# Splitting the first a loads and regrouping the last stores of a batched matmul

## The chip, the cores and the metric

The kernel runs on one core of a Trainium2 chip. The metric is the device time of one execution, in microseconds. The kernel before takes 133.37 us, the median of three runs (133.36, 133.37, 133.55).

## The reference

```python
def setup_inputs():
    return {"a": np.random.randn(1024, 64, 64).astype(np.float32),
            "b": np.random.randn(1024, 64, 64).astype(np.float32)}

def reference(a, b):
    return np.matmul(a, b).astype(np.float32)
```

It is a batch of 1024 products of 64 x 64 matrices. The two inputs are 16.8 MB each, and so is the output, in fp32: 50.3 MB in all for 0.5 GFLOP. The kernel computes in bf16 and accumulates in fp32.

## The kernel before, in words

**Tiles.** The batch is cut into 16 tiles of 64 matrices for b and the output (index t, 1 MB each), and into 8 tiles of 128 matrices for a (index s, 2 MB each, so one a tile serves two t). An a tile is loaded in four parts (h = 0 to 3), each of 32 matrices: a partition holds 16 rows of one matrix, so that four partitions make a matrix, and a part is 128 partitions of 4 KB. In the source the four partitions of a matrix lie 4 KB apart and the next matrix of the part lies 64 KB on. An address pattern for a whole part therefore has an outer dimension of 32 matrices and an inner one of 4.

**Who loads.** For a tiles 1 to 7, GpSimd loads three of the four parts and turns them into bf16 on the way (`cast_load_a`, L73), and SyncE loads the fourth as fp32 (`load_a`, L81). The first a tile is different (`load_first_a`, L84 to L95): all four parts come as fp32, two on SyncE's queue and two on ScalarE's, and land in two buffers of the output pool. A b tile is one load of 1 MB (`load_b`, L100), on SyncE's queue for even t and ScalarE's for odd t, three tiles ahead.

**From a tile to product.** The a tile is cast to bf16 and regrouped (`regroup`, L109 for the first tile, L112 and L115 later; L129 on the path for tiles 1 to 3). It is transposed, on TensorE (`transpose`, L141, copied out by ScalarE in L144) or on VectorE for a tiles 1 to 3 (`transpose_dve`, L131). VectorE then writes it into a block-diagonal operand (`spread`, L157 or L167), so that four matrices share one pass through the 128 x 128 array. The b tile is cast to bf16 (`cast`, L176; the last tile in four pieces, L181 and L183). TensorE multiplies (L221) into PSUM, and ScalarE, with VectorE's help for some tiles, copies the result to an output tile `o_sb` of 128 partitions and 8 KB (`evacuate`, L209). The last tile is multiplied and copied in four quarters, the first and third by ScalarE, the second and fourth by VectorE.

**Stores.** `multiply` does not issue the stores itself: it leaves them in `held`, and `store(t)` issues them one tile later, after the next `multiply` (HOLD is 2). `put(lo, n)` (L198) stores n of the eight column groups of a tile, on the queue that `store_queue` names: GpSimd's for tiles 0 to 14, ScalarE's and SyncE's in turn for tile 15. Tiles 0 to 13 go as one store of 1 MB. Tile 14 goes as two of 512 KB, tile 15 as four of 256 KB.

**What sets the order.** The order is written out by hand (`tc.manual_schedule()`); every engine does its instructions in the order in which the program lists them. At the start SyncE issues two parts of the first a tile, b tile 0, the a_raw part of tile 1, b tile 2 and so on; ScalarE issues two parts of the first a tile, loads its function table, and issues b tile 1; GpSimd issues the three cast loads of a tile 1, builds the identity, clears an operand and goes on to further cast loads. At the end the order is: multiply tile 15, store tile 14, store tile 15. The profile calls GpSimd's DMA queue q0, SyncE's q1 and ScalarE's q10.

Of the kernel before, what the change touches and what calls it, by code (L numbers as in the profile page):

```python
# [13 lines left out]
def kernel(  # L14
# [14 lines left out]
    nc = tc.nc  # L29
# [4 lines left out]
    n_t, n_s = B // 64, B // 128  # L34
# [6 lines left out]
    a_v = a.rearrange("(s g h) (mp v) k -> s h g mp (v k)", h=4, g=32, v=16)  # L41
# [21 lines left out]
    held = {}  # L63

    def store_queue(t, lo):
        if t < n_t - 1:
            return nc.gpsimd
        return nc.scalar if lo % 4 == 0 else nc.sync

    def cast_load_a(s):  # L70
        a_sb = a_pool.tile([128, 3, 16, 64], bf16, name="a_sb")
# [12 lines left out]
    def load_first_a():  # L84

        raw = [
            o_pool.tile([128, 8, 2, 2, 64], fp32, name="o_sb")[:].rearrange(
                "p gh j wl n -> p (gh j wl n)"
            )
            for _ in range(2)  # L90
        ]
        parts = [raw[h % 2][:, 1024 * (h // 2) : 1024 * (h // 2) + 1024] for h in range(4)]
        for h in range(4):
            (nc.scalar if h % 2 else nc.sync).dma_start(out=parts[h], in_=a_v[0, h])  # L94
        a_tiles[0] = parts  # L95

    def load_b(t):
# [92 lines left out]
    def multiply(t):  # L190
        at_bd = bd_tiles[t % N_BD][:].rearrange("p g (j wl) h mp vo -> p j g (wl h mp vo)", j=2)
        at_bd = at_bd.bitcast(bf16).rearrange("p j g (c u) -> p j g c u", u=2)
        b_bf = bbf_tiles.pop(t)
        last = t == n_t - 1
        o_sb = o_pool.tile([128, 8, 2, 2, 64], fp32, name="o_sb")

        def put(lo, n):
            store_queue(t, lo).dma_start(  # L198
                out=o_v[t, :, lo : lo + n, :],
                in_=o_sb[:, lo : lo + n].rearrange("p gh j wl n -> p (gh j wl n)"),  # L200
            )

        def evacuate(o_ps, gh, n, copies):

            for par in range(2):
                for wl in range(2):
                    src = o_ps[64 * wl : 64 * wl + 64, :, par, :, :]
                    dst = o_sb[64 * par : 64 * par + 64, gh : gh + n, :, wl, :]
                    copies[2 * par + wl](dst, src)  # L209

        for half in range(2):
            if not last:
                o_ps = o_psum.tile([128, 4, 2, 2, 64], fp32, name="o_ps")
            for g8 in range(8):
                if last and g8 % 4 == 0:
                    o_ps = t_psum.tile([128, 2, 2, 2, 64], fp32, name="at_ps")
                g = 8 * half + g8
                gl = (g8 % 4 if last else g8) // 2
                for j in range(2):
                    for u in range(2):  # L220
                        nc.tensor.matmul(  # L221
                            o_ps[:, gl, g % 2, j, :],
                            at_bd[:, j, g, :, u],
                            b_bf[:, g, 64 * u : 64 * u + 64],
                            start=(u == 0),
                            stop=(u == 1),
                        )
                if last and g8 % 4 == 3:
                    copy = nc.scalar.copy if g8 == 3 else nc.vector.tensor_copy
                    evacuate(o_ps, g // 4 * 2, 2, [copy] * 4)  # L230
            if not last:
                copies = [nc.scalar.copy] * 4
                if half and t % 2 and t > 2 * max(ON_DVE):
                    copies[2:] = [nc.vector.tensor_copy] * 2
                evacuate(o_ps, 4 * half, 4, copies)
        if last:
            held[t] = [lambda q=q: put(2 * q, 2) for q in range(4)]
        else:
            whole = t < n_t - 2
            held[t] = [lambda q=q: put(q, 8 if whole else 4) for q in ([0] if whole else [0, 4])]  # L240

    with tc.manual_schedule():
        first_cast = cast_load_a(1)
        load_first_a()

        nc.vector.memset(warm[:, 0:1], 0.0)
# [15 lines left out]
        for t in range(n_t):  # L262
            s, half = t // 2, t % 2
            if t + 1 < n_t:
                spread(t + 1)
                cast(t + 1)
            if t + B_AHEAD < n_t:
                load_b(t + B_AHEAD)
            if half == 0 and 0 < s < n_s - 1 - A_AHEAD:
                load_a(s + 1 + A_AHEAD)  # L270
            if half == 0 and 0 < s < n_s - 1 and s + 1 not in ON_DVE:
                transpose(s + 1, 1)
            multiply(t)
            if t == 0:
                transpose_dve(1, 0)
                transpose_dve(1, 1)
                a_tiles.pop(1)
                load_a(A_AHEAD)
                load_a(A_AHEAD + 1)
            if t and s + 2 in ON_DVE and (half or s):  # L280
                for part in [0, 1] if t == 1 else [half]:
                    transpose_dve(s + 2, part)
                if half:
                    a_tiles.pop(s + 2)
            elif half == 0 and 0 < s and s + 2 < n_s:
                regroup(s + 2)
            elif half == 1 and s + 2 < n_s:
                transpose(s + 2, 0)
            if t >= HOLD - 1:
                store(t - HOLD + 1)  # L290
# [32 lines left out]
```

## Time and profile before

| What | Value |
| --- | --- |
| median of three runs | 133.37 us |
| profiled execution, its own time | 133.69 us |
| its span, first to last instruction | 131.8 us |
| HBM read and written | 33.55 MB and 16.78 MB, 382 GB/s over the span |
| busy: TensorE 60.3, VectorE 102.0, ScalarE 88.1, GpSimd 33.2 us | 46%, 77%, 67%, 25% of the span |
| DMA queues q0, q1, q10 | 52.7%, 28.5%, 20.2% of 16 engines' span |
| whole stores of 1 MB, issue to landing | 21.5 us (median of 14) |
| first a loads, issue to landing | 6.8 us on SyncE, 7.5 us on ScalarE (medians of two) |

The span is the time between the first and the last instruction that the profile holds; the execution's own time is longer by what lies around it. "DMA" in the page's slices is the mean busy share of the core's 16 DMA engines, in tenths. A queue's share is the time of its packets over 16 engines' span. GB/s counts what was written, so a load that turns fp32 into bf16 counts half. A DMA is issued by an engine's instruction, and its packets follow later; "landing" is when the last of them has been acknowledged.

### The profile page before, as it was taken

The page shows a single profiled execution, that of the slowest core. Times are in us where ns is not written, and L with a number is a line of the kernel's source. Part 1 is how long each engine was busy: PE and PEld are TensorE (multiplying, and loading weights), DVE is VectorE, ACT ScalarE, POOL GpSimd, SP SyncE. Part 2 cuts the span into 40 slices and gives each one's busy share as a digit, 9 for nine tenths or more (in the row PEclk, how much of TensorE's full clock was granted, in tenths as well). Part 3 has the DMA queues.
Part 4 walks back from the last instruction along what each step waited for, and adds up shares of the span by engine and source line. Part 5 has one row for each costly group of instructions (what it writes and reads, how often), then busy time and mean ns, then how long its engine had stood idle before and what let it go on. Part 6 is the DMA issues. An engine that isn't in the chain of part 4 may idle for free.

```text
span 131.8 us, 2749 instructions
## 1 busy us (share of the span) xinstructions
PE 60.3 (46%) x1104; PEld 57.2 (43%) x1104; DVE 102.0 (77%) x144; ACT 88.1 (67%) x158; POOL 33.2 (25%) x45
## 2 busy tenths in 40 slices
PE   0003701964090270908971983199369615366000
PEld 0003501964090270908961963198368614355000
DVE  5932099807999996999999999599999997798300
ACT  2123605599949069492999989559969998339930
POOL 6991000042016300618120204300420212041200
PEclk9999999999999998555599599559968999679755
DMA  3999999999999999999999999999999999999993
GB/s 71 344 341 306 306 306 297 270 313 319 328 316 401 347 310 308 399 390 395 314 288 364 400 397 359 306 303 389 393 390 392 395 391 393 391 405 402 402 379 135
DMA packets 18252, 44.99 MB, mean 341 GB/s; under 512 B 1088, under 2 KB 2112, under 8 KB 18240
## 3 DMA queue, kind: packets, MB, share of 16 engines
q0 software_dynamic: 7120, 21.24, 52.7%
q1 hardware_dynamic: 6064, 13.63, 28.5%
q10 hardware_dynamic: 5056, 9.96, 20.2%
q8 instruction: 8, 0.13, 0.4%
q14 instruction: 4, 0.03, 0.1%
HBM read 33.55 MB, written 16.78 MB: 382 GB/s over the span
## 4 chain that ended last, share of the span: by engine, by line
DMA 53%; ACT 16%; DVE 14%; PE 6%; issue 5%; SPq 2%; DVEq 0%; ACTq 0%
DMA b_sb<-in_b_dram 53%; ACT o_sb L209 13%; PE o_ps L221 5%; DVE at_bd L167 4%; DVE b_bf L176 4%; DVE at_bd L157 2%; ACT b_bf L176 1%; DVE at_sb L131 1%; DVE o_sb L209 1%; DVE a_bf L112 1%; SPq L94 1%; ACT a_bf L129 1%; SPq L100 1%; ACT b_bf L183 1%; DVE a_bf L115 0%
## 5 line engine op out<-in xcount | busy, mean ns | idle before, releaser
L209 ACT COPY o_sb<-o_ps 64x512 f32<-64x512 f32 x112 | 65.0, 581 | 18.5 <-PE o_ps L221 14.3
L221 PEld LDWEIGHTS <-at_bd 128*128 128x128 bf16 x1024 | 45.3, 117 | 51.5 <-DVE b_bf L176 39.6
L221 PE MATMUL o_ps<-b_bf,at_bd 128*128 128x64 bf16 x960 | 45.7, 223 | 47.1 <-DVE b_bf L176 36.8
L167 DVE COPY at_bd<-at_sb 32x1024 f32<-32x1024 f32 x40 | 29.5, 737 | 5.9 <-ACT at_sb L144 4.9
L198 POOL DMA_DIRECT2D out_dram<-o_sb x16 | 17.1, 1068 | 53.8 <-ACT at_sb L144 21.1
L157 DVE COPY at_bd<-at_sb 32x512 f32<-32x512 f32 x48 | 21.6, 451 | 1.1
L73 POOL DMA_DIRECT2D a_sb<-in_a_dram x21 | 12.0, 588 | 37.2 <-DVE at_sb L131 34.0
L176 DVE CAST b_bf<-b_sb 128x2048 bf16<-128x2048 f32 x14 | 17.4, 1245 | 4.3 <-DMA b_sb<-in_b_dram 4.0
L141 PE MATMUL at_ps<-identity,a_bf 128*128 128x128 f32 x80 | 13.3, 336 | 11.9 <-ACT a_bf L109 11.9
L141 PEld LDWEIGHTS at_ps<-identity,a_bf 128*128 128x128 f32 x80 | 12.2, 181 | 11.9 <-issue 11.9
L144 ACT COPY at_sb<-at_ps 128x512 f32<-128x512 f32 x20 | 10.8, 591 | 2.4 <-PE at_ps L141 2.0
L131 DVE STREAM_TRANSPOSE at_sb<-a_sb 128x512 f32<-128x512 f32 x9 | 8.7, 1055 | 0.0
L131 DVE STREAM_TRANSPOSE at_sb<-a_bf 128x512 f32<-128x512 f32 x3 | 3.1, 1044 | 4.6 <-ACT a_bf L129 4.6
L109 ACT CAST a_bf<-o_sb 128x1024 bf16<-128x1024 f32 x2 | 2.1, 1045 | 5.9 <-DMA o_sb<-in_a_dram 5.9
L209 DVE COPY o_sb<-o_ps 64x512 f32<-64x512 f32 x8 | 5.5, 689 | 0.2
L109 DVE CAST a_bf<-o_sb 128x1024 bf16<-128x1024 f32 x2 | 3.2, 1599 | 2.9 <-DMA o_sb<-in_a_dram 2.9
L176 ACT CAST b_bf<-b_sb 128x2048 bf16<-128x2048 f32 x1 | 1.9, 1899 | 4.5 <-DMA b_sb<-in_b_dram 4.5
L112 DVE COPY a_bf<-a_sb 128x3072 bf16<-128x3072 bf16 x4 | 4.2, 1046 | 0.0
L183 ACT CAST b_bf<-b_sb 128x512 bf16<-128x512 f32 x2 | 1.1, 614 | 4.5 <-DMA b_sb<-in_b_dram 4.5
L250 DVE MEMSET at_bd<- 128x4096 f32 x1 | 3.5, 3472 | 0.8 <-issue 0.8
L209 DVE COPY o_sb<-at_ps 64x256 f32<-64x256 f32 x8 | 3.4, 422 | 0.5 <-PE at_ps L221 0.4
L129 ACT CAST a_bf<-a_raw 128x1024 bf16<-128x1024 f32 x3 | 3.1, 1045 | 0.1
(16 smaller groups left out, 15.4 us busy)
## 6 DMA issues: line engine op xcount, KB each, us to landing
out_dram<-o_sb POOLq DMA_DIRECT2D x14, 1024.0 KB, 21.5
a_sb<-in_a_dram POOLq DMA_DIRECT2D x21, 256.0 KB, 14.2
a_raw<-in_a_dram SPq DMA_DIRECT2D x7, 512.0 KB, 17.5
o_sb<-in_a_dram SPq DMA_DIRECT2D x2, 512.0 KB, 6.8
o_sb<-in_a_dram ACTq DMA_DIRECT2D x2, 512.0 KB, 7.5
out_dram<-o_sb POOLq DMA_DIRECT2D x2, 512.0 KB, 5.9
out_dram<-o_sb SPq DMA_DIRECT2D x2, 256.0 KB, 4.6
out_dram<-o_sb ACTq DMA_DIRECT2D x2, 256.0 KB, 4.6
```

The source lines that it names most:

```text
L73: nc.gpsimd.dma_start(out=a_sb[:, h, :, :].rearrange("p v k -> p (v k)"), in_=a_v[s, h], single_packet=True)
L109: copy(a_bf[:, :, h, :], a_sb[h].rearrange("p (v k) -> p v k", v=16))
L112: nc.vector.tensor_copy(a_bf[:, :, 0:3, :], cast_sb[:].rearrange("p h v k -> p v h k"))
L131: nc.vector.transpose(at_tiles[s][:, h].rearrange("p g w mp vo -> p w vo g mp"), pairs.rearrange("p (vo w kp) -> p w vo kp", vo=4, w=4),)
L141: nc.tensor.transpose(at_ps[:, vo, :], a_cols[:, 4 * vo + 2 * j + wl, :], identity[:])
L144: nc.scalar.copy(at_tiles[s][:, :, 2 * j + wl, :, :], at_ps[:].rearrange("p vo (g mp) -> p g mp vo", mp=4),)
L157: nc.vector.tensor_copy(bd[rows, 8 * i : 8 * i + 8, :, h, :, :].rearrange("p g w mp vo -> p (g w) (mp vo)"), at_sb[block : block + 32, h]. ...
L167: nc.vector.tensor_copy(bd[rows, :, :, h, :, :].rearrange("p g w mp vo -> p (g w) (mp vo)"), at_sb[rows, half].rearrange("p g w mp vo -> p ...
L176: (nc.vector.tensor_copy if t else nc.scalar.copy)(b_bf[:], b_sb[:])
L198: store_queue(t, lo).dma_start(out=o_v[t, :, lo : lo + n, :], in_=o_sb[:, lo : lo + n].rearrange("p gh j wl n -> p (gh j wl n)"),)
L209: copies[2 * par + wl](dst, src)
L221: nc.tensor.matmul(o_ps[:, gl, g % 2, j, :], at_bd[:, j, g, :, u], b_bf[:, g, 64 * u : 64 * u + 64], start=(u == 0), stop=(u == 1),)
```

## The change

It has two parts. At the start, each of the four loads of the first a tile becomes two: the first 8 matrices (32 partitions) and the other 24 (96 partitions), one behind the other on the same queue. At the end, tile 14 is stored whole, in one store of 1 MB on GpSimd's queue, and tile 15 in two: column groups 0 to 5 (768 KB) on GpSimd's queue, groups 6 and 7 (256 KB) on SyncE's. ScalarE issues no store any more.

```diff
     def store_queue(t, lo):
         if t < n_t - 1:
             return nc.gpsimd
-        return nc.scalar if lo % 4 == 0 else nc.sync
+        return nc.gpsimd if lo == 0 else nc.sync
...
         for h in range(4):
-            (nc.scalar if h % 2 else nc.sync).dma_start(out=parts[h], in_=a_v[0, h])
+            queue = nc.scalar if h % 2 else nc.sync
+            for lo, hi in ((0, 8), (8, 32)):
+                queue.dma_start(out=parts[h][4 * lo : 4 * hi], in_=a_v[0, h, lo:hi])
         a_tiles[0] = parts
...
         if last:
-            held[t] = [lambda q=q: put(2 * q, 2) for q in range(4)]
+            held[t] = [lambda: put(0, 6), lambda: put(6, 2)]
         else:
-            whole = t < n_t - 2
-            held[t] = [lambda q=q: put(q, 8 if whole else 4) for q in ([0] if whole else [0, 4])]
+            held[t] = [lambda: put(0, 8)]
```

## The prediction

> **What bounds the kernel now.** I read first the page's 40 slices and its queue table, then the stretches (DMA share and GB/s), the chain, the order of time at both ends, and the queues' packets in short stretches. From the page:
>
> ```profile
> span 131.8 us, 2749 instructions
> DMA  3999999999999999999999999999999999999993
> DMA packets 18252, 44.99 MB, mean 341 GB/s; under 512 B 1088, under 2 KB 2112, under 8 KB 18240
> q0 software_dynamic: 7120, 21.24, 52.7%
> q1 hardware_dynamic: 6064, 13.63, 28.5%
> q10 hardware_dynamic: 5056, 9.96, 20.2%
> DMA 53%; ACT 16%; DVE 14%; PE 6%; issue 5%; SPq 2%; DVEq 0%; ACTq 0%
> ```
>
> The 16 DMA engines are full from the second slice to the last but one; the three queues (q0 GpSimd's, q1 SyncE's, q10 ScalarE's) make up 101% of 16 engines' span. The chain is 53% waits for a b load, and each of those loads is long because it shares the engines. The small packets, 1088, are 16 for each of the kernel's 68 DMAs. The stretches show where the DMA work stops being full:
>
> ```profile
> 2.00:3.00 1.00, 0.00 (x0) 0.00 (x0) 1.00 (x1) 0.67 (x2) 1.00 (x2) 1.00 0.90 152
> 3.00:5.00 2.00, 0.00 (x0) 0.00 (x0) 2.00 (x1) 0.80 (x2) 1.93 (x4) 1.00 0.96 344
> ...
> 121.50:126.50 5.00, 0.00 (x0) 0.00 (x0) 1.69 (x5) 4.84 (x12) 1.40 (x2) 0.71 1.03 398
> 126.50:129.00 2.50, 0.00 (x0) 0.00 (x0) 0.00 (x0) 0.03 (x1) 0.00 (x0) 0.50 1.00 363
> 129.00:130.50 1.50, 0.00 (x0) 0.00 (x0) 0.00 (x0) 0.00 (x0) 0.00 (x0) 0.50 0.53 184
> 130.50:131.80 1.30, 0.00 (x0) 0.00 (x0) 0.00 (x0) 0.00 (x0) 0.00 (x0) 0.50 0.00 0
> ```
>
> The last two columns are the share and GB/s: full until 129, half full until 130.5 (the engines end up to 1.5 us apart), then nothing but closing work. The end in order of time:
>
> ```profile
> 121.39 0.76 POOL L198 DMA_DIRECT2D out_dram<-o_sb  x1 [4.02 <-ACT o_sb L209]
> 121.53 2.13 SPq L198 DMA_DIRECT2D out_dram<-o_sb  x2
> 123.50 1.89 ACT L209 COPY o_sb<-at_ps 64x256 f32<-64x256 f32 x5
> 123.77 0.75 POOL L198 DMA_DIRECT2D out_dram<-o_sb  x1 [1.62 <-ACT o_sb L209]
> 125.40 1.12 ACT L209 COPY o_sb<-at_ps 64x256 f32<-64x256 f32 x3
> 126.55 0.38 ACTq L198 DMA_DIRECT2D out_dram<-o_sb  x1
> ```
>
> The last copy ends at 126.52, the last store is issued at 126.55 and lands 4.2 us later (the DMA issues of that moment), at 130.75; 1.05 us of closing work follow. So the end hangs on two things: bytes still queued, and the last copy. Last, is the limit in each engine or in something they share? Queue rows of 123.5 to 126.5 (all engines busy), then of 129.3 to 130.0 (a third of them idle):
>
> ```profile
> q0 software_dynamic: 225, 0.83, 70.2%
> q1 hardware_dynamic: 370, 0.36, 34.6%
> ```
>
> ```profile
> q10 hardware_dynamic: 170, 0.16, 66.2%
> ```
>
> MB over share of the stretch is the pace at which all 16 engines would go: 0.36/(0.346 x 3.0 us) = 347 GB/s for the 1 KB packets beside others, 0.16/(0.662 x 0.7) = 345 with a third idle. Fewer busy engines are no faster; the limit is each engine's own. GpSimd's 4 KB packets go at 0.83/(0.702 x 3.0) = 394.
>
> **Part 1, the first a tile.** Four loads of 128 rows of 4 KB become eight, of 32 and 96 rows. SP issues two more at about 0.62 us each (1.28 for two), ACT two more at 0.78 (1.56 for two). On SP, load b0 goes from 2.49 to about 3.7 and the a_raw load behind it from 3.27, but that one is held in the queue for 7.69 us anyway. On ACT, b1 goes from 2.76 to 4.3 and the table load from 2.33 to 3.9, done by 5.4, ahead of the cast at 6.46. The a rows keep the engines full until the second pair lands at about 10.6, so the issues cost 0; without that cover they would cost their 1.2 to 1.6 us. No reader starts sooner: the casts (L109) read all 128 partitions and wait for both pieces.
>
> What matters is how the rows are dealt to the engines. The source of a whole load is 32 blocks (one per matrix) of 4 rows; of the pieces, 8 and 24 blocks. Every DMA of the kernel before has an outer count that is a multiple of 16 on both sides, and 16 small packets; a piece with 8 or 24 blocks is the first that can't be dealt evenly in whole blocks. Two ends:
> - Dealt by rows, 32/16 + 96/16 = 8 rows an engine, as now: 0 us.
> - Dealt by blocks, evenly, beginning at the same engine: 8 engines get one block of the first piece (4 rows), 12 get two of the second (8 rows). Eight engines carry 12 rows of each load instead of 8, four carry 8, four none. Over four loads that is 16 packets or 64 KB more on eight engines. At 404 GB/s (the stretch 119 to 122, 4 KB packets alone), 25.3 GB/s an engine, that is 2.6 us; at the 344 of 3 to 5 us, 3.0.
>
> No row decides between these. I take the block dealing, because an even deal with whole blocks is all that the rows show, and count 2.6. In the Trainium skill, page "DMA: Bandwidth & Descriptors", section "Why a DMA increments its semaphore by 16 and not by 1", a DMA from SP or ACT runs on the largest number of engines up to 16 that divides the slowest dimension of both sides, on the lowest-numbered ones: 8 and 12 engines here. By that rule the sum has the 2.6, by the row of 16 small packets read as a constant it has 0.
>
> Would other work hide it? The share is 1.0 or more in every stretch from 3 to 129, and from 129 on some engines stand idle while others still have packets, so rows stay with their engine and lateness on eight engines stays. It shows first in b0: between 6 and 8 us q0, q1 and q10 take turns (67, 70 and 65 packets), 0.50 us for one of each, so 8 more packets on both hardware queues put b0 up to 8 x 0.50 = 4.0 us later, with GpSimd's casts the gainer. Everything behind b0 follows. Low end: if the eight engines are those that end first (up to 1.5 us early), 2.6 - 1.3 = 1.3. Range of part 1: 1.3 to 4.0.
>
> **Part 2, the tail.** Tile 14: two stores of 512 KB (121.39, 123.77) become one of 1 MB at 123.77, when ACT's last copy of the tile is done; its issue takes 0.9 to 1.5 us (the whole stores' rows) instead of 0.75. Before, the engines had some 0.87 MB of older stores at 122 (1.92 MB of q0 from there on, less tile 14's 1.05), 2.2 us of work, so the 512 KB that leave at 123.77 instead of 121.39 open a gap. Tile 15: four stores of 256 KB from SP and ACT (0.38 to 0.40 us each) become 256 KB from SP, at about 123.3 as now, and 768 KB on GpSimd. These wait for ACT's last copy at 126.52, are behind tile 14 in GpSimd's order (issued by 125.3, no cost), and start 0.30 later as at 123.77: 126.82. Nobody waits behind them on GpSimd but the end. ACT's two issues go: 0, its last copy is not behind them.
>
> The unknown is the time from GpSimd's issue to the first packet of a store. Rows: the first cast load is issued at 1.28 and q0 has no packet between 2 and 5, and some between 5 and 6: about 4 us. The store at 121.39 must have come by 124.2, when the older bytes were gone and the share still 1.03: at most 2.8. At least its own issue, about 1.0. I take 2.0, between the two stores' bounds, nearest in kind: first packet 128.8; 786 KB at 394 GB/s, 2.0; last 130.8; landing 0.35 later as now (130.4 to 130.75), 131.15; so +0.4. Tile 14 fits before: 126.0 + 2.66 = 128.7. The 768 KB go at 394 instead of 347, a gain of 0.23 that counts only where no gap is. Ends: -0.2 (no gap) and, at 4 us, +2.4. The Trainium skill, page "DMA: Bandwidth & Descriptors", section "Specifications", gives a first-byte latency of about 1 us for GpSimd's DMAs. By that figure, as an estimate, no gap is left, and the sum would have -0.2 here.
>
> **Sum.** 2.6 + 0.4 = 3.0 us. On the profiled execution: 133.69 (span 131.80 and 1.89 around it) + 3.0 = 136.7. The median of the runs is 0.32 lower, 133.37, so 136.4.
>
> **Rivals.**
> - Even deal: part 1 costs 0, only the tail counts: 133.37 + 0.4 = 133.8. For it: 16 small packets for each DMA before. Against: no DMA before has an outer count of 8 or 24.
> - Late stores: GpSimd's first packet takes 4 us as for the casts at the start. Then the last packets come at 130.8 to 132.8, +2.4: 138.4 with the uneven deal, 135.8 without. For it, the row; against, the tail's bound of 2.8.
> - Faster: the last stores come without a gap, in 4 KB packets. It needs the even deal, and both GpSimd stores' first packet within about 1.3 us of issue (126.82 + 1.3 + 2.0 = 130.1, before the engines that run latest end now); then those engines are never empty before the end and the 0.23 us count: 133.37 - 0.23 = 133.1. For it: the share held 1.03 through both half stores. Against it: the gap's 2.2 us of older bytes, and the 4 us row. The 1 us that the Trainium skill's page "DMA: Bandwidth & Descriptors" has in its section "Specifications" speaks for it.
>
> **How the numbers follow.** Uneven deal with the tail at +0.4: 0.62, own range 133.37 + 1.3 to 133.37 + 4.4, 134.7 to 137.8. Even deal: 0.17 (of it 0.05 within 0.2%). Late stores: 0.09. Faster: 0.12. A change under 0.2% (0.27 us) is about what a measurement of this kernel can't tell. Slower 0.62 + 0.12 + 0.09 = 0.83, same 0.05, faster 0.12. The range takes 133.2 to 137.9, and leaves out the faster case and the late stores with the uneven deal.
>
> **What would show it.** Small packets: 69 DMAs, 1104 with 16 each; with 8 and 12 for the pieces, 61 x 16 + 4 x 20 = 1056. GB/s between 3 and 10 us well under 340, b0's cast 2.6 to 4 us later than 20.71, and the last copy some 2.6 us later than 126.52. In the tail, a share under 1.0 before tile 14's store, and the last landing about 4.3 us after GpSimd's last issue. I am wrong if the page shows 1104, or if the late engines catch up in a stretch that I read as full.

## The result and the profile after

The changed kernel takes 141.33 us, the median of six runs (140.84 to 142.96), against 133.39 us (133.36 to 133.55): 1.0601 times the kernel before, with a 95% interval from 1.0554 to 1.0647. That is 7.9 us, or 6%, slower. The run of 142.96 us counts as slow and is left out of the ratio. The direction was forecast; the size was 2.6 times the forecast 3.0 us and lies outside the range.

First the page of the changed kernel: span, the slices' DMA row, packets and queues.

```profile
span 139.0 us, 2753 instructions
DMA  1999999989999999999999999999999999999594
DMA packets 17644, 44.99 MB, mean 324 GB/s; under 512 B 1056, under 2 KB 1312, under 8 KB 17632
q0 software_dynamic: 7312, 22.02, 52.1%
q1 hardware_dynamic: 5800, 13.37, 27.4%
q10 hardware_dynamic: 4520, 9.44, 19.7%
```

Three things are to be seen. The same 44.99 MB are moved. The small packets are 1056, not 69 x 16 = 1104: the split loads do run on fewer than 16 engines. And the queues' shares, multiplied by the span, give the time for which the 16 engines were at work on packets: 99.2% of 139.0 is 137.9 us, against 101.4% of 131.8, 133.6 us, before (packets of two queues overlap a little, so the sum can pass the span). So 4.3 of the span's 7.2 us are engine time: the same bytes took longer on the engines. The other 2.9 us are time in which engines stood idle. I call the first number the engine time; all runs are compared by it. Where the engines are hardly ever idle, it must grow with the span: it tells where the time went, not why.

The stretches of the changed kernel show where engines were idle (last two columns: share, GB/s):

```profile
2.00:3.00 1.00, 0.00 (x0) 0.00 (x0) 1.00 (x1) 0.00 (x0) 1.00 (x2) 1.00 0.40 86
3.00:5.00 2.00, 0.00 (x0) 0.00 (x0) 2.00 (x1) 0.53 (x2) 1.93 (x4) 1.00 0.90 202
5.00:20.00 15.00, 0.00 (x0) 0.00 (x0) 1.56 (x3) 2.86 (x4) 5.34 (x8) 1.00 1.07 257
...
129.00:131.00 2.00, 0.00 (x0) 0.00 (x0) 0.66 (x2) 1.93 (x6) 0.89 (x1) 1.00 0.41 152
```

At the start, 2 to 3 us, the share is 0.40 where it was 0.90. From 5 to 20 us the engines are as full as before (1.07 and 1.08), yet move 257 GB/s instead of 317. That is the odd row: full engines at a slower pace. The kernel before in this stretch:

```profile
5.00:20.00 15.00, 3.65 (x16) 3.38 (x17) 7.07 (x9) 4.43 (x6) 5.49 (x8) 1.00 1.08 317
```

At the end there is a hole from 129 to 131 us, ahead of tile 14's store.

Last, the order of time: ScalarE's cast of the first b tile, its last copies, and GpSimd's last two stores.

```profile
28.32 1.90 ACT L178 CAST b_bf<-b_sb 128x2048 bf16<-128x2048 f32 x1 [3.78 <-DMA b_sb<-in_b_dram]
...
129.76 3.01 ACT L211 COPY o_sb<-at_ps 64x256 f32<-64x256 f32 x8
130.03 0.89 POOL L200 DMA_DIRECT2D out_dram<-o_sb  x1 [6.25 <-ACT o_sb L211]
...
133.07 0.83 POOL L200 DMA_DIRECT2D out_dram<-o_sb  x1 [2.15 <-ACT o_sb L211]
```

The same cast in the kernel before:

```profile
20.71 1.90 ACT L176 CAST b_bf<-b_sb 128x2048 bf16<-128x2048 f32 x1 [4.54 <-DMA b_sb<-in_b_dram]
```

The first b tile is cast 7.6 us later than before, the last copy ends 6.25 us later (132.77 for 126.52).

### The profile page after: what moved, and what is told of

The parts are those of the page before. It is cut to its first block, busy times and chain, and to the rows that moved or that the text cites. A ratio compares the mean times of both kernels' runs of the same rounds, so it can differ in the third digit from the quotient of the medians.

```text
span 139.0 us, 2753 instructions
## 1 busy us (share of the span) xinstructions
PE 60.7 (44%) x1104; PEld 57.7 (42%) x1104; DVE 100.1 (72%) x144; ACT 88.1 (63%) x158; POOL 33.8 (24%) x45
## 2 busy tenths in 40 slices
DMA packets 17644, 44.99 MB, mean 324 GB/s; under 512 B 1056, under 2 KB 1312, under 8 KB 17632
## 4 chain that ended last, share of the span: by engine, by line
DMA 32%; DVE 30%; ACT 14%; issue 13%; PE 5%; POOL 1%; POOLq 1%; DVEq 0%; SPq 0%
DMA b_sb<-in_b_dram 29%; ACT o_sb L211 11%; DVE at_bd L169 9%; DVE at_bd L159 7%; DVE b_bf L178 6%; PE o_ps L223 5%; DVE at_sb L133 3%; DMA o_sb<-in_a_dram 3%; DVE o_sb L211 2%; ACT a_bf L131 2%; ACT b_bf L178 1%; DVE a_bf L114 1%; DVE a_bf L117 1%; POOL out_dram L200 1%; POOLq L319 1%
## 5 line engine op out<-in xcount | busy, mean ns | idle before, releaser
L200 POOL DMA_DIRECT2D out_dram<-o_sb x16 | 17.9, 1116 | 56.0 <-ACT o_sb L211 26.5
L111 DVE CAST a_bf<-o_sb 128x1024 bf16<-128x1024 f32 x2 | 1.4, 694 | 12.7 <-DMA o_sb<-in_a_dram 12.7
```

The source lines that it names most:

```text
L111: copy(a_bf[:, :, h, :], a_sb[h].rearrange("p (v k) -> p v k", v=16))
L200: store_queue(t, lo).dma_start(out=o_v[t, :, lo : lo + n, :], in_=o_sb[:, lo : lo + n].rearrange("p gh j wl n -> p (gh j wl n)"),)
```

## The experiments

All times are medians. The ratio is to the kernel before, timed beside each run on the same chip (its medians there: 133.52 to 133.65). The last four columns are of the profiled executions.

| Run | us | ratio, 95% interval | span | engine time | first b cast | last copy ends |
| --- | --- | --- | --- | --- | --- | --- |
| kernel before | 133.39 | | 131.8 | 133.6 | 20.71 | 126.52 |
| the change | 141.33 | 1.0601 (1.0554 to 1.0647) | 139.0 | 137.9 | 28.32 | 132.77 |
| loads only, 32 + 96 rows | 139.31 | 1.0435 (1.0410 to 1.0461) | 137.5 | 137.9 | 27.85 | 132.63 |
| tail only | 135.08 | 1.0116 (1.0086 to 1.0146) | 133.3 | 134.1 | 20.84 | 126.49 |
| loads 64 + 64 rows | 136.58 | 1.0219 (1.0193 to 1.0244) | 134.7 | 136.5 | 24.13 | 129.84 |
| loads in two column halves | 135.53 | 1.0150 (1.0112 to 1.0188) | 133.2 | 135.1 | 23.95 | 128.84 |
| 32 extra rows, partitions 0 to 31 | 137.20 | 1.0282 (1.0263 to 1.0300) | 135.2 | 136.1 | 25.47 | 130.42 |
| 32 extra rows, partitions 64 to 95 | 137.66 | 1.0320 (1.0301 to 1.0338) | 135.7 | 136.4 | 25.34 | 129.96 |
| extra whole load | 135.39 | 1.0122 (1.0105 to 1.0139) | 133.8 | 135.4 | 22.91 | 128.11 |
| tile 15's stores only | 134.31 | 1.0071 (1.0043 to 1.0099) | 132.4 | 133.5 | 20.39 | 126.47 |
| tile 14's store only | 133.90 | 1.0032 (1.0008 to 1.0055) | 131.9 | 133.5 | 20.35 | 126.5 |
| before, casts held | 135.99 | 1.0170 (1.0147 to 1.0193) | 134.3 | 135.9 | 19.17 | 125.27 |
| the change, casts held | 142.31 | 1.0646 (1.0620 to 1.0673) | 140.3 | 139.9 | 25.06 | 131.13 |
| column halves, casts held | 137.36 | 1.0272 (1.0249 to 1.0295) | 135.6 | 136.7 | 19.63 | 126.57 |

### The two parts alone

```diff
+            queue = nc.scalar if h % 2 else nc.sync
+            for lo, hi in ((0, 8), (8, 32)):
+                queue.dma_start(out=parts[h][4 * lo : 4 * hi], in_=a_v[0, h, lo:hi])
```

> The split of the first a loads alone, the tail as before. In the changed kernel the last copy ended 6.25 us later than before and the first b tile landed 7.6 us later, so whatever the cause, the split should carry most of the 7.95 us: 139.5 to 140.9. Prediction's step (only the number of rows on the busiest engines counts, 2.6 to 4.0 us): 136.0 to 137.4, and the rest would have to come from the tail.

Measured: 139.31, +5.7 us. The lead that the changed kernel's trace gave holds (139.5 was its lower end), the prediction's step does not. The split alone has all the extra engine time, 137.9 us.

The other run has the change's two edits of `store_queue` and `held`, and whole loads.

> The new tail alone, loads whole. The changed kernel's last landing came 4.87 us after the last copy, 4.23 before, and the closing took 1.36 instead of 1.05: 0.9 us, 134.3. Prediction's step: +0.4, 133.8. If the split's price was the predicted 3 us, the tail would have to be 4 us or more: 137.5.

Measured: 135.08, +1.45 us, which is none of the three forecasts. In the tail alone the share from 123.5 to 126.5 is 0.69, so 0.9 us are lost there; in the change the hole from 129 to 131 has a share of 0.41, 1.2 us in two. The medians of the parts add up to 7.2 of the 7.9 us. In the profiled executions nothing is missing: the spans grow by 5.7 and 1.5 us, together by the change's 7.2. So the 0.8 us may be noise of the medians; no profile shows them.

### Is it the uneven deal, the row split, or the number of DMAs?

```diff
-            for lo, hi in ((0, 8), (8, 32)):
+            for lo, hi in ((0, 16), (16, 32)):
```

> Each load of the first a tile split into 64 and 64 partitions (16 blocks of 4 rows each), tail as before: eight DMAs, but 16 blocks can be dealt evenly over 16 engines, 4 rows an engine and piece. Uneven deal as the whole cause: 133.4, within 0.3. Collision (a piece that does not span all 128 partitions sends two engines to the same partitions, so its packets take longer whatever the deal): 2 MB at 60 to 75% of the pace, +2 to +4 us, 135.5 to 137.5, with packets on q1 and q10 well over 165 ns. Eight DMAs instead of four as the cause: like the split alone, about 140.

Measured: 136.58, +2.95 us, with an even deal. The page and the queues from 6 to 9.5 us (packets, MB, share of 16 engines):

```profile
DMA packets 18316, 45.00 MB, mean 334 GB/s; under 512 B 1152, under 2 KB 2176, under 8 KB 18304
...
q10 hardware_dynamic: 116, 0.39, 39.6%
q1 hardware_dynamic: 102, 0.35, 36.9%
```

The same two queues and stretch in the kernel before:

```profile
q1 hardware_dynamic: 125, 0.50, 37.2%
q10 hardware_dynamic: 126, 0.51, 35.3%
```

1152 is 72 x 16: every DMA ran on 16 engines. But MB over share gives a pace of 0.39/(0.396 x 3.5 us) = 281 GB/s on q10 and 271 on q1, where before it was 413 and 384. The four loads still make 512 packets of 4 KB. The trace's records of single packets give the mean time of one of these: 243 ns on both queues, where it was 168 on ScalarE's and 204 on SyncE's. In the changed kernel, from 8 to 17 us (when the split loads are on their way):

```profile
q1 hardware_dynamic: 346, 0.95, 39.7%
q10 hardware_dynamic: 287, 0.92, 39.1%
```

0.95/(0.397 x 9) = 266 and 0.92/(0.391 x 9) = 261 GB/s: the same slow pace. At the pace of before (1.01 MB in 72.5% of 3.5 us, 398 GB/s) these 1.87 MB would have taken 4.7 us of engine time; they took 78.8% of 9 us, 7.1. So 2.4 us of the price are longer packets on these two queues. They are not the split loads' alone: 346 packets for 0.95 MB are 2.7 KB each, because the first b tiles, in packets of 2 KB, already run behind the rows of 4 KB. By the packet records, the split loads took 1.1 us of engine time more in all than the whole ones (239 ns a packet for 168 on ScalarE's queue, 202 for 204 on SyncE's), and the first two b tiles 1.3 us more (118 and 102 ns a packet for 95 and 84).

The next run has as many DMAs, but cuts the columns and leaves each load with all 128 partitions.

```diff
+            for lo, hi in ((0, 512), (512, 1024)):
+                queue.dma_start(out=parts[h][:, lo:hi], in_=a_v[0, h, :, :, lo:hi])
```

> Each load of the first a tile split into two halves of the columns, 128 partitions each with 2 KB rows, tail as before: eight DMAs, even deal, every engine keeps the rows that it has in the whole load. Uneven deal and collision both say 133.4 to 133.9 (2 KB packets cost a little more). Eight DMAs as the cause: about 140.

Measured: 135.53, +1.9 us, between the two forecasts and a miss for both: half a microsecond at most had been allowed. Its engine time is 1.5 us up and its span 1.4, so this too is engine time and not the issues; its packets of 2 KB are one known difference. A part of the 2.95 us of the row split may therefore have nothing to do with which partitions a piece covers. The next pair of runs changes the partitions without splitting anything, and a table behind it parts the engine time of all these runs.

### Rows on eight engines, and where they are written

Here the four loads stay whole. Ahead of each goes an extra load of 8 blocks of 4 rows into a spare buffer, which nobody reads. The two runs differ in one number, the partition where these rows are written: the diff is that of the first, and in the second `[0:32]` is `[64:96]`.

```diff
+            queue = nc.scalar if h % 2 else nc.sync
+            queue.dma_start(out=extra[h][0:32], in_=a_v[1, h, 0:8])
+            queue.dma_start(out=parts[h], in_=a_v[0, h])
```

> The kernel before with whole loads, and ahead of each of the four an extra load of 8 blocks of 4 rows (32 rows of another a tile, never used) into partitions 0 to 31 of a spare buffer. These go to eight engines, 4 rows each: the same 16 extra packets on eight engines as the change, while the four loads themselves stay evenly dealt. If an engine that writes partitions 4i to 4i+3 keeps to the group that it writes in a whole load, there is no collision: packets at 160 to 175 ns, and the price is the prediction's step alone, 2.6 to 4.0 us: 136.2 to 137.6. The extra 0.5 MB is in that price. Collision theory: the same, 2.6 to 4.0, with short packets. If any load on eight engines slows the others, packets of 200 ns and more, and 138 to 139.

> As the run before, with one number changed: the extra rows go to partitions 64 to 95, which in a whole load belong to other engines than the eight that bring the extra rows. Collision theory: while an extra row is on its way, two engines write the same group of partitions, packets on q1 and q10 are longer than in the run before, and the time is 0.5 to 2 us above it: 137 to 139. Count of rows alone: the same time as the run before, within 0.3 us.

Measured: 137.20 and 137.66. Small packets are 1120 in both pages, 68 x 16 + 4 x 8: the 8 blocks do go to eight engines. The queue of ScalarE from 9.5 to 13 us, first with the rows in partitions 0 to 31:

```profile
q10 hardware_dynamic: 138, 0.47, 33.1%
```

and with the rows in partitions 64 to 95:

```profile
q10 hardware_dynamic: 123, 0.42, 40.2%
```

The pace is 0.47/(0.331 x 3.5) = 406 GB/s in the first and 298 in the second. This is the stretch with the clearest difference; over all 320 packets of 4 KB on this queue the mean is 163 ns in the first and 183 in the second, on SyncE's 186 and 189. Same source rows, same number of engines, same bytes; the destination alone makes the packets longer, and the time by 0.46 us (the intervals, up to 1.0300 and from 1.0301, just part; 0.5 to 2 had been forecast). So both of these are real: 16 more packets on eight engines cost 3.7 us, 0.5 MB of extra rows included, with these loads' packets at their usual pace, and rows written to other partitions cost pace on top. The Trainium skill, page "DMA: Bandwidth & Descriptors", section "The descriptor swizzle", says that in a 128-partition transfer each engine writes partitions of its own, engines 0 to 7 those of the lower half (four from 0 to 31 and four from 32 to 63), engines 8 to 15 the upper half. The pair of runs agrees with it: rows that the first eight engines write to 0 to 31 stay on their own partitions, rows to 64 to 95 go to those of the others. That two engines then get in each other's way is argued; the packet records do not name the engine.

The same 0.5 MB, dealt evenly, and all of it ahead of SyncE's first load:

```diff
+        nc.sync.dma_start(out=spare[:, 0:1024], in_=a_v[1, 0])
         for h in range(4):
             (nc.scalar if h % 2 else nc.sync).dma_start(out=parts[h], in_=a_v[0, h])
```

> The kernel before with one extra whole load (128 rows of 4 KB, never used) ahead of the first on SyncE's queue: the same 0.5 MB as in the two runs with extra rows, but 8 packets on each of 16 engines instead of 16 on each of eight. Full engines as the bound: 8 x 0.16 = 1.3 us, up to 2.0 with the other queues' turns, so 134.8 to 135.6, clearly under the 137.2 of the rows on eight engines. If it is the bytes or the later landing of the loads that costs, and not on whom they fall: 137.2.

Measured: 135.39, +1.74 us, within what full engines give and 1.8 us under the same bytes on eight engines. The span is 2.0 us longer, the engine time 1.8: with an even deal, what is added to the engines is added to the end.

Whose packets became longer can be read from the packet records, by queue and size (us of engine time more than in the kernel before; the sums differ from the table above by up to 0.2):

| Run | first a loads | b loads | all else | sum |
| --- | --- | --- | --- | --- |
| the change | 1.1 | 2.0 | 1.1 | 4.2 |
| loads only, 32 + 96 rows | 1.1 | 2.1 | 1.1 | 4.3 |
| loads 64 + 64 rows | 1.8 | 0.5 | 0.4 | 2.7 |
| loads in two column halves | 0.1 | 0.9 | 0.4 | 1.4 |
| 32 extra rows, partitions 0 to 31 | 1.0 | 0.7 | 0.7 | 2.4 |
| 32 extra rows, partitions 64 to 95 | 1.5 | 0.7 | 0.4 | 2.6 |
| extra whole load | 1.2 | 0.5 | 0.1 | 1.8 |

In the last three rows the first column holds the extra 0.5 MB. This settles what the column halves left open: the 64 + 64 split costs pace in the first loads themselves, the column halves hardly do. Moving the extra rows adds 0.4 us in these loads, about the 0.46 us of the time. And in every run b loads, which no edit touched, take longer too; with 32 + 96 rows that is the largest part.

### Is the late first b tile what carries it?

In all the runs that touch the first a loads the first b tile comes late, and the prediction had it as the carrier. These runs bring it earlier. One GpSimd instruction, which reads one element a partition of that tile, is put ahead of six cast loads, so that they wait for it.

```diff
+    hold = consts.tile([128, 1], fp32)
...
+        nc.gpsimd.tensor_copy(hold[:], b_tiles[0][:, 0, 0:1])
         load_a(2)
```

> The kernel before, with one GpSimd instruction more that reads one element a partition of the first b tile, ahead of the cast loads of a tiles 2 and 3: these six loads wait until the b tile has landed. From 5 to 20 us GpSimd's queue took 47% of the engines' time, some 3.7 us of it for these six. Turns theory (what GpSimd's queue takes in this stretch, the first b tile loses): the b tile is cast 3 to 4 us earlier than 20.7. What that is worth at the end is open, since all bytes still have to be moved: between nothing and 1 us faster, 132.4 to 133.5, if full engines set the end; more than 2 us faster, under 131.5, if the start of the work alone sets it.

> The whole change, with the same hold on the cast loads of a tiles 2 and 3. If the turns that GpSimd's queue takes while eight engines are late are part of the price, the first b tile's cast comes from 28.3 to about 24 and the time falls from 141.3 to 138 to 139.5. If the price is rows and collisions on the two other queues alone, both stay: 28 and 141.

> The loads split into two halves of the columns (135.53, b tile cast at 23.95), with the same hold. Turns theory: a 2 KB packet has the same turn as GpSimd's longer one, so the split gives that queue more of each round; with it held back there is no one to lose to, the b tile's cast comes before 20 and the time to 133 to 134. If the eight issues themselves are the price, the b tile stays late and the time stays at 135.5.

Measured: 135.99, 142.31 and 137.36. The tile came 1.5, 3.3 and 4.3 us earlier, the last copies ended 1.3, 1.6 and 2.3 us earlier, and all three kernels became slower, by 2.4, 1.0 and 1.8 us. All three times are above every forecast made for them. So the turns of GpSimd's queue do delay the first b tile, but an earlier tile and an earlier last copy bought nothing here. What grew is again the engine time, by 2.3, 2.0 and 1.6 us; in the change the time grew by 1.0 us less than that, so what an earlier tile would be worth without longer packets is not shown. For the kernel before with held casts the queues show where. From 15.5 to 18 us, the b loads by themselves:

```profile
q1 hardware_dynamic: 181, 0.37, 54.4%
q10 hardware_dynamic: 178, 0.36, 52.4%
```

The kernel before from 12 to 15 us, the same b loads beside GpSimd's casts:

```profile
q0 software_dynamic: 157, 0.28, 50.1%
q1 hardware_dynamic: 155, 0.32, 30.6%
q10 hardware_dynamic: 158, 0.32, 27.6%
```

By themselves they go at 0.37/(0.544 x 2.5) = 272 and 275 GB/s, beside the casts at 349 and 386. Packets of 2 KB on these two queues account for 1.7 of the 2.3 us. My theory that the late b tile carries the price is not borne out by these runs.

### The tail in two

```diff
-        return nc.scalar if lo % 4 == 0 else nc.sync
+        return nc.gpsimd if lo == 0 else nc.sync
...
-            held[t] = [lambda q=q: put(2 * q, 2) for q in range(4)]
+            held[t] = [lambda: put(0, 6), lambda: put(6, 2)]
```

> Of the change only tile 15's stores (768 KB on GpSimd, 256 KB on SyncE); tile 14 in two halves as before. If the tail's 1.45 us come from the gap that the missing first half opens, this costs 0 to 0.3: 133.4 to 133.9. If they come from the late 768 KB, or from 4 KB packets at 190 instead of 165 ns that were seen in the tail, 0.9 to 1.4: 134.5 to 135.0.

And the other half: `held[t] = [lambda: put(0, 8)]` for tiles 0 to 14, tile 15 in quarters.

> Of the change only tile 14's store, whole instead of halves; tile 15 in four quarters as before. Gap theory: engines that have finished the older stores wait for about 1.5 us after the issue, 0.7 to 1.2 us are lost: 134.3 to 134.8. If the 768 KB are the cause, 0 to 0.3: 133.4 to 133.9.

Measured: 134.31 (+0.8 us), between the two forecasts, and 133.90 (+0.4, of which the interval leaves 0.1 to 0.7), as forecast if the gap is not the cause. The sum of the two is close to the tail's 1.45. The larger share is that of tile 15's stores, so the gap alone, which I had taken for the cause, is the smaller one. The traces show a slower pace. GpSimd's queue alone in the tail-only run, from 129.6 to 131.2 us (tile 15's 768 KB):

```profile
q0 software_dynamic: 136, 0.56, 100.6%
```

The same queue alone in the kernel before, from 118 to 121 us:

```profile
q0 software_dynamic: 316, 1.21, 102.9%
```

0.56/(1.006 x 1.6) is 348 GB/s, 1.21/(1.029 x 3.0) is 392. The late stores, begun on empty queues, go 11% slower than the backlog before them. Why is not shown.

## Why the prediction was wrong, point by point

- **The bound.** Right: full engines set the end. The evenly dealt kernels show it best, with span and engine time up by 2.0 and 1.8, 2.9 and 2.9, 1.4 and 1.5 us. The pace that I took from it was wrong, below.
- **The issues, 0.** Right. SP's four took 3.31 us and ACT's four 3.70, more than the forecast 2.5 and 3.1; b0 was issued at 4.66 and had its turn long after. The column halves have as many issues: from 2 to 5 us their engines work 2.81 us, before 2.82. (In the change it is 2.20: 0.6 us lost at the start, with first pieces that reach eight engines.)
- **The deal: 8 and 12 engines.** Right, and exact: 1056 small packets, as forecast. With it the rival of the even deal falls. In the Trainium skill, page "DMA: Bandwidth & Descriptors", section "Why a DMA increments its semaphore by 16 and not by 1", the number of engines is the largest up to 16 that divides the slowest dimension of both sides; 1056, 1120 and 1152 agree with it for 8, 12 and 16.
- **Sixteen more packets on eight engines, 2.6 us.** Right for the packets themselves, which kept their 163 ns on ScalarE's queue. The run that has this term without a split measured 3.7 us (under the upper end of 4.0), but its engine time rose by 2.5 us where 128 more packets of 163 ns make 1.3: the rest is longer packets elsewhere, 0.7 of it in b loads.
- **The step that failed: the packets' time.** "Fewer busy engines are no faster; the limit is each engine's own" was read from stores whose rows lie as they always do. From it I priced the 16 extra packets at 162 ns and put a change in all others at nothing. The runs show in its place that a packet's time changes with what else is on its way and where it is written: the split alone costs 5.7 us of span, of which only 1.4 are idle engines and 4.3 are longer packets for the same bytes, 1.1 in the split loads, 2.1 in b loads and 1.1 in others. That the destination can do this is shown by the pair of runs with extra rows; that it is the reason in the 32 + 96 and 64 + 64 splits is argued, since there the deal of rows to engines changed with it. Why the b loads, on their old queues and with their old shapes, are slower behind the split loads stays open.
- **What is late next.** I had b0 late by up to 4.0 us, and wrote "Everything behind b0 follows". It was 7.6 us late. That its lateness costs the time is not borne out: brought 1.5 to 4.3 us earlier, with longer packets in exchange, it gained nothing at the end.
- **The tail, +0.4.** Undersized: 1.45 alone. The first packet came sooner than assumed: in the change q0 has none between 130.5 and 131.5 us and some right after, 1.5 us from the issue at 130.03, not 2.0, which would have made it -0.1. What I missed is the pace of 348 GB/s where I had counted 394 (0.26 us for 768 KB, 0.35 for 1 MB), and that SyncE's 256 KB came too late to fill the gap: in the tail-only run they were issued at 124.52 and shared the engines with tile 14 after it.
- **The rivals.** The late stores (first packet after 4 us, as for the casts at the start) did not happen; nor did the faster one. The 4 us were no fixed delay of GpSimd's issue either: with the first cast load issued at 1.28 us each time, q0's first packet came at 5.24 us in the kernel before, at 3.39 in the change and at 2.80 with its loads alone.

No version among these beats the kernel before. It stays open why extra rows to partitions 64 to 95, b loads without a third queue beside them, and stores begun on empty queues are slower.

## What to carry to other kernels

Before a load is cut in pieces, look at the outer count of both sides of each piece: 8 or 24 blocks do not reach 16 engines, and the count of small packets in the page shows what was done. A cut along the partitions can make packets longer even where the deal stays even (64 + 64: 2.95 us for nothing); add up packets' time over the queues, not only bytes, and compare it with the span, then see whose packets grew: here they were not only those of the loads that were cut. In this kernel, whose engines are nearly always full, an earlier first tile was worth nothing once the order of the transfers made packets longer.

## What the runs showed of the hardware, unexpected

- A 4 KB load packet is not of one price: on ScalarE's queue 168 ns on average in whole loads, 239 in the 32 + 96 pieces, 243 in the 64 + 64 pieces, and 183 instead of 163 when only the destination of some extra rows was moved from partitions 0 to 31 to 64 to 95.
- Packets of other loads grow with them: the first b tile's 2 KB packets took 118 ns behind the split loads, 95 before.
- The b tiles were faster beside another queue: 349 and 386 GB/s beside GpSimd's casts, 272 and 275 by themselves.
- GpSimd's stores moved 392 GB/s out of a backlog and 348 when they began on empty queues.
- From issue to first packet, a GpSimd store of 1 MB took 1.5 us; the first cast load took 4.0 us in the kernel before and 1.5 with the loads split, from the same issue time.
